# S5 batches of a hybrid decoder step: which engine turns the chunk contributions, and from where

## The chip, the cores and the metric

The kernel runs on one core of a Trainium2 chip. The metric is the device time of one execution, in microseconds (us). All data are fp32; the large products split each operand into a rounded high part and a low rest and take three matmuls per tile.

## The reference

One layer for 1024 prompt tokens and 32 sample tokens: a modulated input goes through `w_in` into five parts; one feeds an RG-LRU, one an S5 state space model, two are gates; then the merge, a norm, a SwiGLU and a norm. The S5 branch, which the change touches, is this (64 groups of 16 channels, 64 complex states each; chunks of the sequence are chained by a scan):

```python
    def body(carry, u_blk):
        hr, hi = carry
        br = jnp.einsum('blgq,gpq->blgp', u_blk, bb_re)
        bi = jnp.einsum('blgq,gpq->blgp', u_blk, bb_im)
        br = br.at[:, 0].add(a_re * hr - a_im * hi)
        bi = bi.at[:, 0].add(a_re * hi + a_im * hr)
        ...
        _, _, xr, xi = lax.associative_scan(_clin_op, (ar, ai, br, bi), axis=1)
        y = jnp.einsum('blgp,gqp->blgq', xr, c_re) - jnp.einsum('blgp,gqp->blgq', xi, c_im)
        return (xr[:, -1], xi[:, -1]), y
```

## The kernel before, in words

**Ticks.** The order of all work is written out by hand. `product` (L346) walks over three column blocks of 352; for each it calls `tick()`, which first runs whatever is due in this tick, then sends 24 matmuls (L342) and hands the PSUM bank to an evacuation. In the stage in question the products are those of `w_in` for the S5 input (evacuated at L456) and for the two gates (evacuated at L861 into one buffer, which a DMA stores).

**The S5 batches.** Eight batches of eight groups run beside these products, on all engines. `S5_PLAN` (L829) lists their steps with the tick in which each is due; batch b begins at tick 3 + 6b, so a new batch starts every six ticks and up to three are under way. Per batch: `s5_const1`, `s5_const2` and `s5_pre1` to `s5_pre4` make the tables and the turned weights (`s5_pre4`: transposes on TensorE L720, copies on ScalarE L722); `s5_turn1` and `s5_turn2` make the table `ee` of a rotation, beginning with ScalarE's L698, and `s5_pe1` (L710, copied at L712) a kernel; `s5_pe2` (L748) makes the chunk contributions, real and imaginary for four pairs of groups, 136 columns each (128 chunks of the prompt, 8 of the samples), in three PSUM banks, which ScalarE copies into `ww` (L751). `s5_rot_in` multiplies them by the rotation's two parts (GpSimd one, VectorE the other), so that a real scan on VectorE (`s5_scan`, L774) can follow; `s5_rot_out` turns the scan's result back in the same way. `s5_states` makes the states, lets ScalarE copy the last of each (`fin`, L793, L794) and stores the others by four DMAs into the operand `xs5` of `s5_pe3` (L811, L812), whose banks `s5_gelu1` and `s5_gelu2` work on.

**Helpers.** All `TENSOR_TENSOR` rows stand at line L117 and all `SCALAR_TENSOR_TENSOR` rows at L126. The split of a weight tile into its two parts is ScalarE's L230 and a GpSimd subtraction (`weights_t<-small_t,weights_t`). In the trace `s_t` and `left_t` are the two memory regions of this stage (`tq`, in which GpSimd's products land, lies in `left_t`; `ww`, `vv`, `ee` in `s_t`), and `ps` is PSUM.

**Banks.** `bank()` hands out the eight PSUM banks in turn. Six ticks take 15: six for products, three each for `s5_pe2` and `s5_pe3`, two for `s5_pre4`, one for `s5_pe1`. The product in the second tick after `s5_pe2`'s tick gets the first bank of `s5_pe2` again.

Of the kernel before, what the change touches and what calls it, by code (L numbers as in the profile page):

```python
# [12 lines left out]
AF = mybir.ActivationFunctionType  # L13
OP = mybir.AluOpType
# [57 lines left out]
def tile_hawk_s5(ctx: ExitStack, tc: tile.TileContext, io):  # L72
    nc = tc.nc
    V, A, P, PE, SP = nc.vector, nc.scalar, nc.gpsimd, nc.tensor, nc.sync
# [50 lines left out]
    def stt(e, out, a, s, b, op0, op1):  # L125
        e.scalar_tensor_tensor(out, a, s, b, op0=op0, op1=op1)  # L126
# [21 lines left out]
    o = 0  # L148
# [15 lines left out]
    fin = cst(2, 32)  # L164
# [263 lines left out]
    s5m = {}  # L428
# [22 lines left out]
    def z_s5_evac(j):  # L451
        def evac(nb, b):
            ze = s5m[f"ze{j % 2}"]
            bias = C["b_in"][:, 16 + j:17 + j]
            n = 44 if nb < 2 else 40
            A.activation(ze[:, :, 8 + 44 * nb:8 + 44 * nb + n].rearrange("p s c -> p c s"),  # L456
                         b[:, :8 * n].rearrange("p (c s) -> p c s", s=8), AF.Identity, bias=bias)
            if nb == 2:
                zs = b[:, 320:352].rearrange("p (q i) -> p i q", i=4)
                A.activation(ze[:, 0:4, 0:8], zs, AF.Identity, bias=bias)  # L460
                A.activation(ze[:, 4:8, 136:144], zs, AF.Identity, bias=bias)
                for s in range(8):
# [274 lines left out]

    groups = ((0, 3), (3, 6), (6, 8))

    def s5_pe2(b):  # L740

        wt, ub, ww = s5m["wt"], s5m["ub"][b % 2], s5m["ww"]
        for n0, n1 in groups:
            wb_ = bank()
            for n in range(n0, n1):
                r, pr = divmod(n, 4)
                for h in range(2):
                    PE.matmul(wb_[64 * h:64 * h + 64, 136 * (n - n0):136 * (n - n0) + 136],  # L748
                              wt[:, 2 * pr + h, 64 * r:64 * r + 64], ub[:, 2 * pr + h, 8:144],
                              start=True, stop=True, skip_group_check=True)  # L750
            A.activation(ww[:, n0:n1], sub(wb_, n1 - n0, 136), AF.Copy)  # L751

    def s5_rot_in(b):

        ww, ws, ee, vv, tq, tv = (s5m[n] for n in ("ww", "ws", "ee", "vv", "tq", "tv"))
        w4 = ww.rearrange("p (r n) c -> p r n c", r=2)
        t = sub(tq, 2, 4, 128)
        for r in (1, 0):
            tt(P, t[:, r], w4[:, r, :, :128], ee[:, 1], OP.mult)
            tt(V, vv[:, r], w4[:, r, :, :128], ee[:, 0], OP.mult)  # L760

    def s5_scan(b):
        ww, ws, vv, tq, tv = (s5m[n] for n in ("ww", "ws", "vv", "tq", "tv"))
        w4 = ww.rearrange("p (r n) c -> p r n c", r=2)
        wf = ww.rearrange("p n c -> p (n c)")
        t = sub(tq, 2, 4, 128)
        A.activation(ws[:, :, 4 * b:4 * b + 4, :], w4[:, :, :, 128:], AF.Copy)
        rr = sub(tv, 4, 128)
        A.activation(rr, over(r8[:, 4 * b:4 * b + 4, None], 4, 128), AF.Copy)
        P.memset(rr[:, :, 0:1], 0.0)  # L770
        tt(V, vv[:, 0], vv[:, 0], t[:, 1], OP.add)
        tt(V, vv[:, 1], vv[:, 1], t[:, 0], OP.subtract)
        for r in range(2):
            V.tensor_tensor_scan(wf[:, 512 * r:512 * r + 512], tv[:, :512],  # L774
                                 vv[:, r].rearrange("p n c -> p (n c)"), 0.0, op0=OP.mult, op1=OP.add)

    def s5_rot_out(b):
        ww, ee, vv, tq, xs5, x0s = (s5m[n] for n in ("ww", "ee", "vv", "tq", "xs5", "x0s"))
        x0s = x0s[b % 2]
        x4 = sub(ww.rearrange("p n c -> p (n c)"), 2, 4, 128)  # L780
        t = sub(tq, 2, 4, 128)
        for r in (1, 0):
            tt(P, t[:, r], x4[:, r], ee[:, 1], OP.mult)
            tt(V, vv[:, r], x4[:, r], ee[:, 0], OP.mult)
        A.activation(xs5[:64, :, 0:8], x0s[:64], AF.Copy)
        A.activation(xs5[64:, :, 0:8], x0s[64:], AF.Copy, scale=-1.0)

    def s5_states(b):
        vv, tq, xs5 = (s5m[n] for n in ("vv", "tq", "xs5"))
        t = sub(tq, 2, 4, 128)  # L790
        tt(V, vv[:, 0], vv[:, 0], t[:, 1], OP.subtract)
        stt(V, vv[:, 1], vv[:, 1], -1.0, t[:, 0], OP.mult, OP.subtract)
        A.activation(fin[:, 0, 4 * b:4 * b + 4], vv[:, 0, :, 127], AF.Copy)  # L793
        A.activation(fin[:, 1, 4 * b:4 * b + 4], vv[:, 1, :, 127], AF.Copy, scale=-1.0)  # L794
        xg = xs5.rearrange("p (n h) c -> p h n c", h=2)
        for r in range(2):
            for h in range(2):
                SP.dma_start(xg[64 * r:64 * r + 64, h, :, 9:136], vv[64 * h:64 * h + 64, r, :, 0:127])

    y_banks = {}  # L800

# [21 lines left out]
    def s5_gelu2(b):  # L823
        gel = s5m["gel"]
        for n0, n1, yv in y_banks.pop(b):
# [3 lines left out]
    S5_PLAN = ((-3, s5_load), (1, s5_const1), (1, s5_pre1), (1, s5_pre2), (2, s5_pre3),  # L829
               (2, s5_load2), (2, s5_const2), (5, s5_turn1), (5, s5_turn2), (5, s5_pe1),  # L830
               (6, s5_k), (6, s5_pre4), (7, s5_pe2), (8, s5_rot_in), (8, s5_toeplitz),
               (9, s5_scan), (10, s5_rot_out), (11, s5_states), (14, s5_pe3), (15, s5_gelu1),
               (16, s5_gelu2))

    def s5_batch(b, first):
# [20 lines left out]
    def merge_evac(d, j, m, st=None):  # L856
        st = s5m["stage"] if st is None else st

        def evac(nb, b):
            s = slice(352 * nb, 352 * nb + 352)  # L860
            A.activation(st[:, s], b[:, :NB], AF.Tanh, bias=bh[:, m - 24:m - 23], scale=0.5)  # L861
            if nb == 2:
                SP.dma_start(d[j], st)
        return evac
# [17 lines left out]
    for k in range(8):  # L882
# [14 lines left out]
        if k in W2_K:  # L897
            i = W2_K.index(k)
# [14 lines left out]
    for j in range(2):  # L913
        e = z_s5_evac(j)
# [48 lines left out]
    def zl_evac(j):  # L963
        def evac(nb, b):
            bias = C["b_in"][:, j:j + 1]
            zs = zl[:, 1027:1083].rearrange("p (s i) -> p s i", i=7)
            n = 352 if nb < 2 else 320
            if nb == 0:
                P.memset(zl[:, 0:3], 0.0)
                P.tensor_copy(zs[:, :, 0:3], C["conv0"][:, j])  # L970
            A.activation(zl[:, 3 + 352 * nb:3 + 352 * nb + n], b[:, :n], AF.Identity, bias=bias)
            if nb == 2:
                ts(V, zs[:, :, 3:7], seqs(b[:, 320:352]), bias, op0=OP.add)
            later(2, lru_conv, j, nb)
            later(3, lru_split, j, nb)
        return evac
# [114 lines left out]
    e = merge_evac(d_tb, 7, 39, zl[:, :T])  # L1091
# [53 lines left out]
    def lru_out_evac(j):  # L1145
        t, m_ = ta_t[j % 2], mo_t[j % 2]

        def evac(nb, b):
            s = slice(352 * nb, 352 * nb + 352)
            stt(V, m_[:, s], t[:, s], 1.0, b[:, :NB], OP.add, OP.mult)  # L1150
            if nb == 2:
                SP.dma_start(d_m[j], m_)
        return evac

    y_load(0)
    for j in range(8):
# [4 lines left out]
        w, e = use_w("lru", j), lru_out_evac(j)  # L1161
# [410 lines left out]
    n1, n2 = plan.emit(1)  # L1572
# [79 lines left out]
    n = len(UNITS)  # L1652
    for u, (j, ss) in enumerate(UNITS):
        bk = {s: {"set": s if len(ss) > 1 else u % 2} for s in ss}
        for v in range(7):
            for s in ss:
# [4 lines left out]
                w, x = parts[7 * u + v], operand(v, s)  # L1661
# [35 lines left out]
    for c, (k0, k1) in enumerate(DOWN[:-1]):  # L1697
        for m in range(8):
# [37 lines left out]
    ws = [next_w("down", (LASTK, m)) for m in range(8)]  # L1736
    for q in ORDQ:
        for m in range(8):
# [3 lines left out]
            b = bank()  # L1742
# [7 lines left out]
    x = M[0]  # L1750
# [150 lines left out]
```

## Time and profile before

| what | value |
|---|---|
| median of 3 runs | 1831.78 us (1830.85 to 1835.74) |
| the profiled execution | 1828.24 us, its span 1826.5 us |
| busy in the span | TensorE 95%, its weight loads 92%, VectorE 64%, ScalarE 39%, GpSimd 56% |
| granted TensorE clock over the span | 0.978 |
| the stage of the S5 batches | about 92 to 376 us of the span |

The shares are averages over stages with different limits. The stage of the S5 batches is a sixth of the span. How its engines wait for one another is read from its own stretch, batch by batch.

### The profile page before, as it was taken

Reading aid. Unit: us, or ns where it says so; the run is one execution under the profiler, and the core shown is the slowest. Engines: PE = TensorE matmul, PEld = TensorE weight load, DVE = VectorE, ACT = ScalarE, POOL = GpSimd, SP = SyncE. Lnnn points to the kernel's source line nnn. Section 1 sums busy time; section 2 is a strip of 40 time slices with the busy share of each in tenths; the row PEclk is TensorE's granted clock in tenths of the full one; section 3 lists DMA queues with packets and bytes.
Section 4 is the critical chain, followed back from the end, with each engine's and each line's share of the span. In section 5 each row is a group of like instructions: output and inputs, shape, how many; then the busy total and the mean of one; then the engine's idle time right before and its main releaser. Section 6 shows DMA issues by size and latency. Waiting matters only on the chain.

```text
span 1826.5 us, 33873 instructions
## 1 busy us (share of the span) xinstructions
PE 1726.6 (95%) x13380; PEld 1687.1 (92%) x13380; DVE 1161.9 (64%) x1946; ACT 719.0 (39%) x1448; POOL 1021.5 (56%) x839
## 2 busy tenths in 40 slices
PE   6999999999878889999999998999999999999996
PEld 5989889999878889999999998999999999999996
DVE  6989999837888853322677577345455545543588
ACT  4433333325555453222345355335433332211244
POOL 3566656435765742255758725567777675222654
PEclk9999999999989999999999999999999999999998
DMA  9335444432111129765344433432233225932212
GB/s 352 102 106 150 155 130 146 142 111 74 61 40 51 49 79 243 233 234 203 114 163 148 135 105 106 139 119 95 95 126 110 95 95 225 368 125 75 82 35 62
DMA packets 118639, 240.93 MB, mean 132 GB/s; under 512 B 23120, under 2 KB 62288, under 8 KB 115408
## 3 DMA queue, kind: packets, MB, share of 16 engines
q1 hardware_dynamic: 118480, 238.76, 39.5%
q8 instruction: 105, 1.72, 0.4%
q14 instruction: 54, 0.44, 0.1%
HBM read 179.59 MB, written 54.97 MB: 128 GB/s over the span
## 4 chain that ended last, share of the span: by engine, by line
PE 64%; DVE 14%; POOL 9%; issue 6%; DMA 3%; ACT 2%; SPq 0%; POOLq 0%; DVEq 0%; ACTq 0%
PE ps L1174 36%; PE ps L342 13%; PE ps L1693 12%; DVE s_t L117 7%; POOL weights_t L117 3%; POOL r_t L117 3%; POOL lru_t L117 2%; DVE left_t L117 1%; DVE s_t L774 1%; DVE rear_t L117 1%; DMA ada_w_t<-in_w_ada_dram 1%; PE ps L401 1%; DVE s_t L126 1%; DMA small_t<-in_w_in_dram 1%; PE ps L748 1%
## 5 line engine op out<-in xcount | busy, mean ns | idle before, releaser
L1174 PE MATMUL ps<-r_t,weights_t 128*128 128x264 f32 x5496 | 683.4, 285 | 10.4 <-POOL weights_t L117 7.9
L1174 PEld LDWEIGHTS ps<-r_t,weights_t 128*128 128x128 f32 x5496 | 672.6, 188 | 16.8 <-POOL weights_t L117 9.9
L117 POOL TENSOR_TENSOR weights_t<-small_t,weights_t 128x512 fp32r<-128x512 f32 (+3 forms) x312 | 395.5, 1283 | 438.1 <-ACT weights_t L230 358.9
L342 PE MATMUL ps<-r_t,weights_t 128*128 128x352 f32 x3384 | 574.1, 330 | 1.5 <-ACT weights_t L230 1.1
L342 PEld LDWEIGHTS ps<-r_t,weights_t 128*128 128x128 f32 x3384 | 556.5, 194 | 11.2 <-issue 7.3
L230 ACT ACTIVATE weights_t<-small_t 128x512 fp32r<-128x512 f32 (+3 forms) x286 | 151.4, 572 | 245.8 <-PE ps L1693 95.3
L126 DVE SCALAR_TENSOR_TENSOR rear_t<-ps,small_t,rear_t 128x264 f32<-128x264 f32 (+1 forms) x192 | 92.5, 482 | 122.8 <-PE ps L1693 95.4
L1693 PE MATMUL ps<-r_t,weights_t 128*128 128x264 f32 x1344 | 166.3, 286 | 4.1 <-ACT weights_t L230 3.3
L1693 PEld LDWEIGHTS ps<-r_t,weights_t 128*128 128x128 f32 x1344 | 165.1, 190 | 5.2 <-ACT weights_t L230 3.5
L117 DVE TENSOR_TENSOR small_t<-ps,small_t 128x264 f32<-128x264 f32 (+1 forms) x228 | 84.8, 379 | 102.4 <-ACT small_t L1618 74.5
L126 DVE SCALAR_TENSOR_TENSOR rear_t<-rear_t,ps 128x264 f32<-128x264 f32 (+1 forms) x74 | 33.2, 457 | 174.1 <-PE ps L1174 95.2
L117 DVE TENSOR_TENSOR s_t<-s_t 128x128 f32<-128x128 f32 (+3 forms) x200 | 134.3, 719 | 11.5 <-ACT s_t L751 5.8
L117 POOL TENSOR_TENSOR r_t<-rear_t,r_t 128x264 fp32r<-128x264 f32 (+2 forms) x77 | 96.9, 1262 | 59.5 <-ACT r_t L1189 22.7
L117 DVE TENSOR_TENSOR rear_t<-rear_t,small_t 128x32 f32<-128x32 f32 (+3 forms) x137 | 97.3, 719 | 41.0 <-POOL weights_t L117 30.9
L117 POOL TENSOR_TENSOR rear_t<-rear_t,small_t 128x264 f32<-128x264 f32 (+1 forms) x108 | 90.9, 863 | 54.6 <-ACT small_t L1237 44.3
L117 POOL TENSOR_TENSOR weights_t<-rear_t,weights_t 128x512 fp32r<-128x512 f32 x57 | 75.2, 1323 | 55.9 <-ACT weights_t L1534 55.9
L126 DVE SCALAR_TENSOR_TENSOR lru_t<-lru_t 128x1056 f32<-128x1056 f32 (+1 forms) x52 | 81.8, 1574 | 29.7 <-ACT lru_t L1012 16.3
L117 POOL TENSOR_TENSOR r_t<-small_t,r_t 128x528 fp32r<-128x528 f32 (+1 forms) x58 | 78.7, 1366 | 35.8 <-ACT r_t L209 25.8
L1693 PE MATMUL ps<-r_t 128*128 128x264 f32 x768 | 96.7, 286 | 0.8 <-POOL r_t L117 0.8
L1693 PEld LDWEIGHTS ps<-r_t 128*128 128x128 f32 x768 | 94.6, 188 | 1.7 <-POOL r_t L117 1.2
L126 DVE SCALAR_TENSOR_TENSOR lru_t<-lru_t,small_t 128x352 f32<-128x352 f32 (+2 forms) x96 | 87.9, 915 | 3.4
L117 POOL TENSOR_TENSOR left_t<-s_t 128x512 f32<-128x512 f32 (+1 forms) x40 | 76.9, 1944 | 5.9 <-DVE s_t L117 3.5
(225 smaller groups left out, 1920.5 us busy)
## 6 DMA issues: line engine op xcount, KB each, us to landing
d_f<-r_t SPq DMA_DIRECT2D x44, 528.0 KB
r_t<-d_f SPq DMA_DIRECT2D x22, 1056.0 KB
small_t<-in_w_up_dram SPq DMA_DIRECT2D x43, 512.0 KB
small_t<-in_w_in_dram SPq DMA_DIRECT2D x40, 512.0 KB
small_t<-in_w_ada_dram SPq DMA_DIRECT2D x32, 512.0 KB
small_t<-in_w_glu_dram SPq DMA_DIRECT2D x32, 512.0 KB
ada_w_t<-in_w_ada_dram SPq DMA_DIRECT2D x16, 512.0 KB
small_t<-in_w_out_dram SPq DMA_DIRECT2D x16, 512.0 KB
```

What stands on the lines that cost most here:

```text
L117: e.tensor_tensor(out, a, b, op=op)
L126: e.scalar_tensor_tensor(out, a, s, b, op0=op0, op1=op1)
L230: A.activation(self.hi[:, s], self.raw[:, s], AF.Copy)
L342: PE.matmul(out[:, :NB], a[:, k, :], x[:, h, nb, k, :], start=bool(first and n == 0 and q == 0), stop=bool(last and n == len(kts) - 1 and ...
L401: PE.matmul(b[32 * j:32 * j + 32, :128], silu_c[:, 2 * i + k, :], w.raw[:, k, 128 * j:128 * j + 128], start=i == k == 0, stop=i == 3 and k ...
L748: PE.matmul(wb_[64 * h:64 * h + 64, 136 * (n - n0):136 * (n - n0) + 136], wt[:, 2 * pr + h, 64 * r:64 * r + 64], ub[:, 2 * pr + h, 8:144], ...
L774: V.tensor_tensor_scan(wf[:, 512 * r:512 * r + 512], tv[:, :512], vv[:, r].rearrange("p n c -> p (n c)"), 0.0, op0=OP.mult, op1=OP.add)
L1174: PE.matmul(out[:, :Q], a[:, k, :], x(h, k), start=bool(first and n == 0 and q == 0), stop=bool(last and n == len(kts) - 1 and q == 2), sk ...
L1693: PE.matmul(b[:, :Q], a[:, n, :], f[:, h, Q * q:Q * q + Q], start=n == i == 0, stop=k == k1 - 1 and i == 2)
```

## The change

Three things in the S5 branch. `s5_pe2` no longer copies its banks to `ww`; ScalarE copies only the eight sample columns of each into `ws` (L756 of the changed kernel), and `s5_rot_in` has VectorE multiply the other 128 columns straight from the banks. So that real and imaginary parts lie as a bank needs them, the banks hold the pairs (real 0 to 2), (imaginary 0 to 2) and (real 3, imaginary 3). `s5_rot_out` puts its two products of GpSimd on VectorE. And the copies of the final states become a step of their own, `s5_fin`, due at tick 12 in place of 11.

```diff
     def s5_pe2(b):
 
-        wt, ub, ww = s5m["wt"], s5m["ub"][b % 2], s5m["ww"]
-        for n0, n1 in groups:
+        wt, ub, ws = s5m["wt"], s5m["ub"][b % 2], s5m["ws"]
+        w_banks[b] = []
+        for i, pairs_ in enumerate((((0, 0), (0, 1), (0, 2)), ((1, 0), (1, 1), (1, 2)), ((0, 3), (1, 3)))):
             wb_ = bank()
-            for n in range(n0, n1):
-                r, pr = divmod(n, 4)
+            for n, (r, pr) in enumerate(pairs_):
                 for h in range(2):
-                    PE.matmul(wb_[64 * h:64 * h + 64, 136 * (n - n0):136 * (n - n0) + 136],
+                    PE.matmul(wb_[64 * h:64 * h + 64, 136 * n:136 * n + 136],
                               wt[:, 2 * pr + h, 64 * r:64 * r + 64], ub[:, 2 * pr + h, 8:144],
                               start=True, stop=True, skip_group_check=True)
-            A.activation(ww[:, n0:n1], sub(wb_, n1 - n0, 136), AF.Copy)
+            x = sub(wb_, len(pairs_), 136)
+            w_banks[b].append(x[:, :, :128])
+            dst = ws[:, i, 4 * b:4 * b + 3, :] if i < 2 else ws[:, :, 4 * b + 3, :]
+            A.activation(dst, x[:, :, 128:], AF.Copy)
 
     def s5_rot_in(b):
...
-        for r in (1, 0):
-            tt(P, t[:, r], w4[:, r, :, :128], ee[:, 1], OP.mult)
-            tt(V, vv[:, r], w4[:, r, :, :128], ee[:, 0], OP.mult)
+        for i, x in enumerate(w_banks.pop(b)):
+            for o, e in ((t, 1), (vv, 0)):
+                if i < 2:
+                    tt(V, o[:, i, :3], x, ee[:, e, :3], OP.mult)
+                else:
+                    tt(V, o[:, :, 3], x, over(ee[:, e, 3, None, :], 2, 128), OP.mult)
 
     def s5_scan(b):
...
-        A.activation(ws[:, :, 4 * b:4 * b + 4, :], w4[:, :, :, 128:], AF.Copy)
...
@@ s5_rot_out
         for r in (1, 0):
-            tt(P, t[:, r], x4[:, r], ee[:, 1], OP.mult)
+            tt(V, t[:, r], x4[:, r], ee[:, 1], OP.mult)
             tt(V, vv[:, r], x4[:, r], ee[:, 0], OP.mult)
...
@@ s5_states
-        A.activation(fin[:, 0, 4 * b:4 * b + 4], vv[:, 0, :, 127], AF.Copy)
-        A.activation(fin[:, 1, 4 * b:4 * b + 4], vv[:, 1, :, 127], AF.Copy, scale=-1.0)
...
+    def s5_fin(b):
+        vv = s5m["vv"]
+        A.activation(fin[:, 0, 4 * b:4 * b + 4], vv[:, 0, :, 127], AF.Copy)
+        A.activation(fin[:, 1, 4 * b:4 * b + 4], vv[:, 1, :, 127], AF.Copy, scale=-1.0)
...
-               (9, s5_scan), (10, s5_rot_out), (11, s5_states), (14, s5_pe3), (15, s5_gelu1),
+               (9, s5_scan), (10, s5_rot_out), (11, s5_states), (12, s5_fin), (14, s5_pe3), (15, s5_gelu1),
```

VectorE's order at the turn in of a batch, as a difference (the last of `s5_const1` above it, the first of `s5_const2` below):

```order
 L117 TENSOR_TENSOR s_t<-left_t,small_t 128x128 x2
 L117 TENSOR_TENSOR s_t<-s_t 128x128
-L117 TENSOR_TENSOR s_t<-s_t 128x512 x2
+L117 TENSOR_TENSOR left_t<-ps,s_t 128x384
+L117 TENSOR_TENSOR s_t<-ps,s_t 128x384
+L117 TENSOR_TENSOR left_t<-ps,s_t 128x384
+L117 TENSOR_TENSOR s_t<-ps,s_t 128x384
+L117 TENSOR_TENSOR left_t<-ps,s_t 128x2x128
+L117 TENSOR_TENSOR s_t<-ps,s_t 128x2x128
 L117 TENSOR_TENSOR left_t<-left_t,s_t 128x1152
```

Six products that read a PSUM bank stand where two that read SBUF stood; at the turn out, likewise, four 512-column products on VectorE stand for two.

GpSimd's order over one batch, from the memset of one scan (L770) to that of the next, before:

```order
L770 MEMSET s_t 128x4
L117 TENSOR_TENSOR weights_t<-small_t,weights_t 128x512 x2
L117 TENSOR_TENSOR left_t<-s_t 128x512 x2
L117 TENSOR_TENSOR weights_t<-small_t,weights_t 128x512 x2
L117 TENSOR_TENSOR s_t<-s_t 128x1024
L117 TENSOR_TENSOR left_t<-s_t 128x1024
L117 TENSOR_TENSOR left_t<-s_t 128x512 x2
L117 TENSOR_TENSOR s_t<-s_t,left_t 128x1024
L770 MEMSET s_t 128x4
```

and in the changed kernel:

```order
L775 MEMSET s_t 128x4
L117 TENSOR_TENSOR weights_t<-small_t,weights_t 128x512 x4
L117 TENSOR_TENSOR s_t<-s_t 128x1024
L117 TENSOR_TENSOR left_t<-s_t 128x1024
L117 TENSOR_TENSOR s_t<-s_t,left_t 128x1024
L775 MEMSET s_t 128x4
```

The four 512-column products of the turns are gone; `s5_pre1`, `s5_pre2` and `s5_pre3` (the three of 1024 columns) now follow one another directly.

ScalarE's order from the evacuation of tick 10 to L722, before:

```order
L861 ACTIVATE left_t<-ps,small_t 128x352
L793 ACTIVATE small_t<-s_t 128x4
L794 ACTIVATE small_t<-s_t 128x4
L698 ACTIVATE s_t<-left_t 128x8x16
L712 ACTIVATE s_t<-ps 128x2x128
L861 ACTIVATE left_t<-ps,small_t 128x352
L722 ACTIVATE s_t<-ps 128x512 x2
```

and in the changed kernel:

```order
L869 ACTIVATE left_t<-ps,small_t 128x352
L698 ACTIVATE s_t<-left_t 128x8x16
L712 ACTIVATE s_t<-ps 128x2x128
L869 ACTIVATE left_t<-ps,small_t 128x352
L805 ACTIVATE small_t<-s_t 128x4
L806 ACTIVATE small_t<-s_t 128x4
L722 ACTIVATE s_t<-ps 128x512 x2
```

The two copies of the final states (L793 and L794 before, L805 and L806 now) moved behind L698, L712 and an evacuation; they still stand ahead of L722.

## Rows read from the trace of the kernel before

**Rows 1.** Chain of waits, 180 to 262 us, its shares by line.

```profile
by line: DVE s_t L117 51.8%; issue 15.6%; DVE left_t L117 14.2%; DVE s_t L774 12.4%; DVE s_t L126 6.6%; ACT s_t L698 0.7%; POOL s_t L770 0.3%; POOLq L117 0.2%; DVEq L117 0.1%; POOLq L770 0.1%; ACT small_t L794 0.1%; ACTq L861 0.0%
```

**Rows 2.** Stretches of a batch: length; busy PE, PEld, DVE, ACT, POOL; PEclk; DMA.

```profile
155.56:187.66 32.10, 30.60 (x234) 29.64 (x233) 31.25 (x42) 10.63 (x29) 21.70 (x11) 1.00 0.52 154
...
257.65:291.90 34.25, 32.27 (x233) 31.14 (x232) 33.19 (x46) 12.32 (x33) 21.57 (x12) 0.95 0.46 145
...
sum 239.37, PE 222.69 PEld 214.63 DVE 226.19 ACT 87.80 POOL 144.38; mean PE 31.81 PEld 30.66 DVE 32.31 ACT 12.54 POOL 20.63
```

**Rows 3.** Waits of TensorE, 92 to 376 us: total, times, longest.

```profile
PE ps L748 <- ACT s_t L722: 14.4, 7, 2.7
...
PE ps L720 <- DVE s_t L126: 1.9, 2, 1.3
PE ps L812 <- DMA s_t<-s_t: 1.5, 2, 1.1
```

**Rows 4.** Waits of VectorE, 92 to 376 us.

```profile
DVE s_t L117 <- ACT s_t L698: 3.3, 7, 0.5
```

**Rows 5.** Timeline of TensorE in two batches: start, length, and idle time before.

```profile
166.45 2.10 PE L748 MATMUL ps<-s_t 128*64 128x136 f32 x32 [1.50 <-ACT s_t L722]
...
262.96 4.08 PE L342 MATMUL ps<-r_t,weights_t 128*128 128x352 f32 x24
269.02 2.67 PE L748 MATMUL ps<-left_t,s_t 128*64 128x136 f32 x32 [1.98 <-ACT s_t L722]
271.62 5.09 PE L342 MATMUL ps<-r_t,weights_t 128*128 128x352 f32 x24
```

**Rows 6.** Timeline, 228 to 256 us: turn out, turn in, `s5_const2`, a product.

```profile
228.43 3.32 DVE L117 TENSOR_TENSOR s_t<-s_t 128x512 f32<-128x512 f32 x2
...
243.91 3.11 DVE L117 TENSOR_TENSOR s_t<-s_t 128x512 f32<-128x512 f32 x2
244.07 2.40 POOL L117 TENSOR_TENSOR left_t<-s_t 128x1024 f32<-128x1024 f32 x1 [0.23 <-DVE s_t L117]
...
246.02 11.70 PE L342 MATMUL ps<-r_t,weights_t 128*128 128x352 f32 x72
...
246.94 2.44 DVE L117 TENSOR_TENSOR left_t<-left_t,s_t 128x1152 f32<-128x1152 f32 x1
...
250.50 3.50 POOL L117 TENSOR_TENSOR s_t<-s_t,left_t 128x1024 f32<-128x1024 f32 x1
251.78 3.43 DVE L117 TENSOR_TENSOR left_t<-left_t,s_t 128x1152 f32<-128x1152 f32 x1
...
255.14 1.40 DVE L126 SCALAR_TENSOR_TENSOR s_t<-s_t,ps 128x408 f32<-128x408 f32 x3
```

**Rows 7.** Timeline: VectorE alone, and reading PSUM beside GpSimd's split.

```profile
84.14 1.35 DVE L117 TENSOR_TENSOR s_t<-left_t,s_t 128x1152 f32<-128x1152 f32 x1
...
222.31 1.28 DVE L117 TENSOR_TENSOR s_t<-s_t,left_t 128x512 f32<-128x512 f32 x2
...
226.08 2.19 POOL L117 TENSOR_TENSOR weights_t<-small_t,weights_t 128x512 fp32r<-128x512 f32 x1
227.12 1.39 DVE L126 SCALAR_TENSOR_TENSOR s_t<-s_t,ps 128x408 f32<-128x408 f32 x3
```

**Rows 8.** Line L117, 765 to 1550 us: ns at least, median and most.

```profile
L117 DVE TENSOR_TENSOR small_t<-ps,small_t x191: 176/433/437, 1026.8 to 1549.2; 128x264 f32<-128x264 f32 x180, 128x32 f32<-128x32 f32 x11
...
L117 DVE TENSOR_TENSOR small_t<-small_t,rear_t x28: 434/436/1498, 884.7 to 1068.8; 128x264 f32<-128x264 f32 x28
```

**Rows 9.** Timeline of ScalarE, 230 to 237 us.

```profile
232.58 0.21 ACT L793 ACTIVATE small_t<-s_t 128x4 f32<-128x4 f32 x1 [4.64 <-DVE s_t L117]
...
233.30 0.29 ACT L698 ACTIVATE s_t<-left_t 128x128 f32<-128x128 f32 x1
...
234.20 1.08 ACT L722 ACTIVATE s_t<-ps 128x512 f32<-128x512 f32 x2
```

**Rows 10.** Busy time just behind the stage.

```profile
375.00:408.00 33.00, 33.00 (x226) 32.58 (x224) 16.50 (x31) 10.12 (x23) 9.16 (x11) 1.00 0.30 107
```

More of the change, by code (lines that the diff above doesn't have):

```diff
@@ L738, in tile_hawk_s5 @@
     groups = ((0, 3), (3, 6), (6, 8))
+    w_banks = {}
     def s5_pe2(b):
-        wt, ub, ww = s5m["wt"], s5m["ub"][b % 2], s5m["ww"]
-        for n0, n1 in groups:
+        wt, ub, ws = s5m["wt"], s5m["ub"][b % 2], s5m["ws"]
+        w_banks[b] = []
+        for i, pairs_ in enumerate((((0, 0), (0, 1), (0, 2)), ((1, 0), (1, 1), (1, 2)), ((0, 3), (1, 3)))):
             wb_ = bank()
-            for n in range(n0, n1):
-                r, pr = divmod(n, 4)
+            for n, (r, pr) in enumerate(pairs_):
                 for h in range(2):
-                    PE.matmul(wb_[64 * h:64 * h + 64, 136 * (n - n0):136 * (n - n0) + 136],
+                    PE.matmul(wb_[64 * h:64 * h + 64, 136 * n:136 * n + 136],
                               wt[:, 2 * pr + h, 64 * r:64 * r + 64], ub[:, 2 * pr + h, 8:144],
                               start=True, stop=True, skip_group_check=True)
-            A.activation(ww[:, n0:n1], sub(wb_, n1 - n0, 136), AF.Copy)
+            x = sub(wb_, len(pairs_), 136)
+            w_banks[b].append(x[:, :, :128])
+            dst = ws[:, i, 4 * b:4 * b + 3, :] if i < 2 else ws[:, :, 4 * b + 3, :]
+            A.activation(dst, x[:, :, 128:], AF.Copy)
     def s5_rot_in(b):
-        ww, ws, ee, vv, tq, tv = (s5m[n] for n in ("ww", "ws", "ee", "vv", "tq", "tv"))
-        w4 = ww.rearrange("p (r n) c -> p r n c", r=2)
+        ee, vv, tq = (s5m[n] for n in ("ee", "vv", "tq"))
         t = sub(tq, 2, 4, 128)
-        for r in (1, 0):
-            tt(P, t[:, r], w4[:, r, :, :128], ee[:, 1], OP.mult)
-            tt(V, vv[:, r], w4[:, r, :, :128], ee[:, 0], OP.mult)
+        for i, x in enumerate(w_banks.pop(b)):
[4 more added lines that the diff above has]
+                    tt(V, o[:, :, 3], x, over(ee[:, e, 3, None, :], 2, 128), OP.mult)
     def s5_scan(b):
-        ww, ws, vv, tq, tv = (s5m[n] for n in ("ww", "ws", "vv", "tq", "tv"))
-        w4 = ww.rearrange("p (r n) c -> p r n c", r=2)
+        ww, vv, tq, tv = (s5m[n] for n in ("ww", "vv", "tq", "tv"))
         wf = ww.rearrange("p n c -> p (n c)")
         t = sub(tq, 2, 4, 128)
-        A.activation(ws[:, :, 4 * b:4 * b + 4, :], w4[:, :, :, 128:], AF.Copy)
         rr = sub(tv, 4, 128)
```

## The prediction

> **What bounds the kernel now.** The page's shares (TensorE 95%, VectorE 64%) say little here, since the change lies in one stage only: the 61 ticks in which TensorE works off products of `w_in` while the eight batches of the S5 branch run beside them, from about 92 to 376 us. So I read that stage, in four steps.
>
> First the chain of waits inside it. From 180 to 262 us it hardly touches TensorE: nearly nine tenths are VectorE's lines, and most of the rest is "issue" [rows 1]. So in this stage VectorE sets the pace, not TensorE.
>
> Then the period of one batch (six ticks), taken from one `s5_pe1` on TensorE to the next. It is 34.25 us at 257.65, of which VectorE is busy for 33.19, and the seven periods in a row sum to 239.37 [rows 2]. The cheapest one, at 155.56, is 32.10 us at a granted clock of 1.00, with one wait of 1.50 in it [rows 2, 5]. Without that wait TensorE needs **30.6 us** per batch: that is its floor.
>
> Third, where TensorE loses the difference. It waits in front of `s5_pe2` (L748) for ScalarE's copy of the turned weights (L722): 14.4 us in seven waits, beside 1.9 us at L720 and 1.5 us at L812 [rows 3]. A second loss follows the wait in five of the seven periods: after 1.98 us of idling the 32 matmuls of L748 take 2.67 instead of 2.10 and the next product 5.09 instead of 4.08 [rows 5], with a mean granted clock of 0.95 in that period against 1.00 [rows 2]. [...] That is 1.6 us each time. Seven floors are 7 x 30.6 = 214.2, so the seven periods hold 239.37 - 214.2 = 25.2 us that VectorE causes; with the 1.1 us or so at the last `s5_pe3` (of the 1.5 at L812) some **26.3 us** are to be had. No more: then TensorE is at its own work.
>
> Fourth, why ScalarE is late and why VectorE is slow. ScalarE stands for 4.64 us at L793, the copy of the final states, until VectorE has made them; L698, L712 and L722 queue behind it, so L722 starts at 234.20 [rows 9]. VectorE is slow because GpSimd holds it up: while GpSimd's 1024-column product runs from 244.07 for 2.40, two 512-column products on VectorE take 3.11 from 243.91 [rows 6]; two of that size with no GpSimd work beside them take 1.28 [rows 7]. But a VectorE instruction that reads one operand from PSUM isn't held: three of them go through in 1.39 from 227.12 while GpSimd's from 226.08 lasts until 228.27 [rows 7], and over 191 PSUM products in the later stages the longest is 437 ns, where the same shape from SBUF has a median of 436 and a longest of 1498 [rows 8].
>
> **The change part by part**, per batch, in VectorE's time.
>
> Turn in (`s5_rot_in`). Before: from 243.91 to 246.94, 3.0 us, for two products, GpSimd doing two others [rows 6]. After: six products from PSUM, 2 x (384 + 384 + 256) columns. The trio of 408, 408 and 272 columns takes 1.39 [rows 7], so 1024 of 1088 columns make 1.31, twice 2.6 us. Gain 0.4. That they aren't held is the step I rest on; if they were, one hold by a 1024-column GpSimd product, 3.11 - 1.28 = 1.8, comes back. Ends: gain 0.4, loss 1.4; I take the gain, by rows 7 and 8.
>
> `s5_const2` behind it. Before: three 1152-column products take from 246.94 to 255.14, 8.2 us, each with a hold: two by GpSimd's turn-in products, one by `s5_pre3` (250.50, 3.50) [rows 6]. Alone, one takes 1.35 at 84.14 [rows 7], three about 3.9. After, GpSimd's queue has nothing between `s5_pre2` and `s5_pre3`, so the latter, 3.50 - 1.28 = 2.2 of own work (from 250.50 it waits until VectorE is through with its second, at 251.78), can hold one of them at most: 3.9 + 2.2 = 6.1. Gain 2.1; ends 0 (all held as now) and 4.3 (`s5_pre3` done in time).
>
> Turn out (`s5_rot_out`). Before: 3.32 us from 228.43, for two products and two holds [rows 6]. After: four at 1.28 per two [rows 7], 2.5. Gain 0.8. If the weight split's two GpSimd products now fall beside them, about 1.1 each is lost.
>
> Final states a tick later. `s5_turn1` no longer waits for L698 behind L793: 3.3 us in seven waits [rows 4], 0.5 per batch. L805 and L806 now stand just ahead of L722, so L722 still waits for the states, but L698, L712 and one evacuation are out of its way: from 233.30 to 234.20, 0.9 us [rows 9].
>
> ScalarE's three copies of `ww` (some 1.3 us) and L767 become three copies of a few columns. ScalarE isn't the bound: nothing in the sum. GpSimd loses four products: nothing either, but for the holds above.
>
> Sum: 0.4 + 2.1 + 0.8 + 0.5 = 3.8 us, so VectorE's period falls from 34.2 to **30.4**, just under TensorE's 30.6. TensorE then sets the pace. One link keeps VectorE from drawing far ahead: `s5_const2` writes the buffer `vx` that `s5_pe3` of the same tick still reads. It costs nothing while TensorE is the bound.
>
> The banks of `s5_pe2` are held longer: VectorE frees them, not ScalarE. TensorE takes the first of them again for the product two ticks on. VectorE began its turn in at about 243.91, and that product starts about 249.8 (a third of the 72 matmuls that take 11.70 from 246.02) [rows 6]: room for 2.6 us of work.
>
> Of the 26.3 us I give back one wait of the present mean size, 14.4 / 7 = 2.1 us, for the first batches, where VectorE starts late, as an estimate: 24.2. The profiled execution took 1828.24, so 1804.0; the median of the runs stands 3.5 above it: 1831.78 - 24.2 = **1807.6 us**.
>
> [...] For 264 columns the rows show no surcharge: median 433 ns from PSUM, 436 from SBUF [rows 8]. [...]
>
> **The rivals.**
> *VectorE stays the bound.* If one hold stays (a PSUM product held after all, or both split products beside the turn out), VectorE's period is 30.4 + 2.0 = 32.4. Saved: 7 x 1.8 + 1 = 14 us, 1818. With both it is 34.4 and nothing is saved. For it: the two engines' periods differ by 0.2 only. Against: rows 8.
> *Given back.* The stage ends earlier, and something that doesn't move takes it all. From 375 to 408 TensorE is busy for 33.00 of 33.00 us [rows 10] with loads well ahead, so I see no such thing; 1831.
> *Slower.* The holds don't go with GpSimd's products: VectorE finds the remaining ones (`s5_pre1` to `s5_pre3`, four of the split) in its way as long as now, while it has 2.6 us more of its own work: two more products of 0.64 and 2.6 - 1.3 for the turn in. With 0.5 for L698 off, its period is 34.2 + 2.1 = 36.3, and seven of them make 15 us: 1847. It decides where the holds that vanish are worth under 2.1 us per batch; by the terms above they are 8.2 - 6.1 = 2.1 in `s5_const2`, 3.32 - 1.28 = 2.0 in the turn out and 1.8 in the turn in, 5.9 in all.
>
> **How the numbers follow.** TensorE at its floor, 1802 to 1812: 0.72. VectorE still the bound, 1812 to 1824: 0.17. Given back: 0.06. Slower: 0.05. Under 0.3%, 5.5 us, a measurement of this kernel can't be told from no change: faster 0.89, same 0.06, slower 0.05. The range from 1801 to 1820 takes in the first case and two thirds of the second.
>
> **What would show it.** Right: periods of 30.6 to 31 us between `s5_pe1` groups, L748's wait gone, granted clock 1.00, six PSUM products at 0.4 to 0.56 us each, one hold among the three 1152-column products. Wrong: PSUM products of 2 us and more, the split beside the turn out, periods over 32, or a new TensorE wait for VectorE at the product two ticks after `s5_pe2`.

## The result, and the profile after

The changed kernel takes **1803.93 us** (median, 1802.32 to 1806.26) against 1831.32 for the kernel before on the same chip: a ratio of 0.9849 (95% interval 0.9826 to 0.9872), 1.5% faster. The forecast was 1807.6 in a range of 1801 to 1820. The execution that was profiled took 1803.03 us, its span 1801.3, against 1828.24 and 1826.5 before.

Stretches of a batch in the changed kernel, from one `s5_pe1` to the next (columns as in [rows 2]); the seventh holds the end of the batches:

```profile
121.08:151.56 30.48, 30.48 (x234) 29.64 (x233) 29.69 (x50) 13.54 (x34) 13.77 (x9) 1.00 0.56 142
151.56:182.04 30.48, 30.48 (x233) 29.64 (x232) 29.02 (x51) 11.36 (x30) 13.39 (x10) 1.00 0.57 162
...
243.01:273.50 30.49, 30.49 (x233) 29.65 (x232) 28.97 (x52) 11.16 (x30) 12.62 (x9) 1.00 0.55 159
...
sum 213.15, PE 213.15 PEld 207.48 DVE 194.70 ACT 80.82 POOL 84.87; mean PE 30.45 PEld 29.64 DVE 27.81 ACT 11.55 POOL 12.12
```

TensorE is busy in every one of the 213.15 us; the seven periods of [rows 2] took 239.37 and held 222.69 us of its work, in five of them at a mean granted clock of 0.95. Now the granted clock is 1.00 in all seven. So 26.2 us are gone between the two `s5_pe1` that bound the sums. In the first six periods VectorE was busy for 33.2 us each before, and is for 29.2 now. Before, these six sum to:

```profile
sum 205.41, PE 190.68 PEld 183.55 DVE 199.21 ACT 74.25 POOL 129.48; mean PE 31.78 PEld 30.59 DVE 33.20 ACT 12.38 POOL 21.58
```

The chain of waits, 180 to 262 us, of which VectorE's lines were 85% [rows 1], is now:

```profile
by line: PE ps L342 74.1%; PE ps L750 7.3%; PE ps L819 6.8%; PE ps L820 6.6%; PE ps L720 3.2%; PE ps L710 2.1%
```

All of it is TensorE's own work. Of TensorE's waits from 92 to 376 us one is left, at the start of the stage, where the kernel before has one of 4.4:

```profile
PE ps L710 <- DVE s_t L117: 4.5, 1, 4.5
```

None of the three groups of waits that cost the kernel before its time [rows 3] has a row any more. VectorE waits instead; its waits from 155 to 300 us:

```profile
DVE s_t L117 <- ACT s_t L698: 2.9, 3, 1.5
DVE left_t L117 <- PE ps L820: 2.0, 3, 0.9
DVE s_t L117 <- PE ps L820: 0.3, 1, 0.3
```

The second and third are the link through `vx` that the forecast named: `s5_const2` writes what `s5_pe3` (L819, L820 now) still reads. The place that decides, the turn in and `s5_const2` behind it, with GpSimd's work beside them, against [rows 6]; and further up in the same batch what became of the holds at the weight split (rows of VectorE and GpSimd alone; a hold is an instruction of VectorE that is drawn out by GpSimd's work beside it):

```profile
223.15 3.00 POOL L117 TENSOR_TENSOR weights_t<-small_t,weights_t 128x512 fp32r<-128x512 f32 x2 [8.74 <-ACT weights_t L230]
...
223.76 1.25 DVE L117 TENSOR_TENSOR s_t<-s_t 128x128 f32<-128x128 f32 x1
...
228.38 0.29 DVE L117 TENSOR_TENSOR s_t<-s_t 128x128 f32<-128x128 f32 x1
228.59 0.55 DVE L117 TENSOR_TENSOR left_t<-ps,s_t 128x384 f32<-128x384 f32 x1
228.75 2.03 POOL L117 TENSOR_TENSOR left_t<-s_t 128x1024 f32<-128x1024 f32 x1 [0.55 <-DVE s_t L117]
229.06 0.55 DVE L117 TENSOR_TENSOR s_t<-ps,s_t 128x384 f32<-128x384 f32 x1
...
230.45 0.41 DVE L117 TENSOR_TENSOR left_t<-ps,s_t 128x256 f32<-128x256 f32 x1
230.78 0.41 DVE L117 TENSOR_TENSOR s_t<-ps,s_t 128x256 f32<-128x256 f32 x1
230.86 2.39 POOL L117 TENSOR_TENSOR s_t<-s_t,left_t 128x1024 f32<-128x1024 f32 x1
231.67 2.80 DVE L117 TENSOR_TENSOR left_t<-left_t,s_t 128x1152 f32<-128x1152 f32 x1 [0.47 <-PE ps L820]
234.39 1.35 DVE L117 TENSOR_TENSOR s_t<-left_t,s_t 128x1152 f32<-128x1152 f32 x1
235.77 1.36 DVE L117 TENSOR_TENSOR left_t<-left_t,s_t 128x1152 f32<-128x1152 f32 x1
237.05 1.41 DVE L126 SCALAR_TENSOR_TENSOR s_t<-s_t,ps 128x408 f32<-128x408 f32 x3
```

The six PSUM products run from 228.59 to about 231.2, 2.6 us, while GpSimd's 1024-column product (`s5_pre2`, 228.75) runs beside them from end to end: none is held. Of the three 1152-column products one is held, by `s5_pre3` (230.86); from the first to the next instruction is 5.4 us, 8.2 before; 0.47 us of waiting for `s5_pe3` stand ahead of it. The weight split (223.15) now stands beside the small products of `s5_const1`: one of 128 columns takes 1.25 us there, where another of the same size takes 0.29 at 228.38. That hold has moved, not gone: before, it lay at `s5_turn1` and `s5_turn2`, which took 6.8 us up to `s5_const1` and take 4.7 in this batch.

### The profile page after: what moved, and what is told of

The parts are those of the page before. It is cut to its first block, busy times and chain, and to the rows that moved or that the text cites. A ratio compares the mean times of both kernels' runs of the same rounds, so it can differ in the third digit from the quotient of the medians.

```text
span 1801.3 us, 33909 instructions
## 1 busy us (share of the span) xinstructions
PE 1718.6 (95%) x13380; PEld 1681.3 (93%) x13380; DVE 1131.2 (63%) x1994; ACT 711.6 (40%) x1440; POOL 954.9 (53%) x807
## 4 chain that ended last, share of the span: by engine, by line
PE 73%; POOL 9%; DVE 7%; issue 5%; DMA 2%; ACT 2%; SPq 0%; POOLq 0%; DVEq 0%; ACTq 0%
PE ps L1182 36%; PE ps L342 20%; PE ps L1701 12%; POOL weights_t L117 3%; POOL r_t L117 3%; POOL lru_t L117 2%; DVE rear_t L117 2%; DVE s_t L117 1%; PE ps L750 1%; PE ps L820 1%; PE ps L819 1%; PE ps L401 1%; DVE small_r_t L486 1%; DMA small_t<-in_w_down_dram 1%; DVE small_t L117 1%
## 5 line engine op out<-in xcount | busy, mean ns | idle before, releaser
L1182 PE MATMUL ps<-r_t,weights_t 128*128 128x264 f32 x5496 | 683.8, 285 | 10.2 <-POOL weights_t L117 6.7
L117 POOL TENSOR_TENSOR weights_t<-small_t,weights_t 128x512 fp32r<-128x512 f32 (+3 forms) x312 | 395.0, 1281 | 472.4 <-ACT weights_t L230 387.3
L342 PE MATMUL ps<-r_t,weights_t 128*128 128x352 f32 x3384 | 569.5, 328 | 1.9 <-ACT weights_t L230 1.1
L342 PEld LDWEIGHTS ps<-r_t,weights_t 128*128 128x128 f32 x3384 | 551.6, 192 | 10.8 <-issue 7.1
L117 DVE TENSOR_TENSOR small_t<-ps,small_t 128x264 f32<-128x264 f32 (+1 forms) x228 | 84.7, 378 | 102.3 <-ACT small_t L1626 74.5
L126 DVE SCALAR_TENSOR_TENSOR rear_t<-rear_t,ps 128x264 f32<-128x264 f32 (+1 forms) x74 | 33.3, 457 | 173.5 <-PE ps L1182 96.7
L117 POOL TENSOR_TENSOR r_t<-rear_t,r_t 128x264 fp32r<-128x264 f32 (+2 forms) x77 | 96.7, 1260 | 59.4 <-ACT r_t L1197 22.7
L117 DVE TENSOR_TENSOR rear_t<-rear_t,small_t 128x32 f32<-128x32 f32 (+3 forms) x137 | 97.3, 719 | 41.1 <-POOL weights_t L117 31.0
L117 POOL TENSOR_TENSOR rear_t<-rear_t,small_t 128x264 f32<-128x264 f32 (+1 forms) x108 | 90.7, 862 | 54.6 <-ACT small_t L1245 44.3
L117 POOL TENSOR_TENSOR weights_t<-rear_t,weights_t 128x512 fp32r<-128x512 f32 x57 | 75.3, 1326 | 56.2 <-ACT weights_t L1542 49.0
L117 POOL TENSOR_TENSOR r_t<-small_t,r_t 128x528 fp32r<-128x528 f32 (+1 forms) x58 | 78.7, 1367 | 35.9 <-ACT r_t L209 26.0
L1701 PE MATMUL ps<-r_t 128*128 128x264 f32 x768 | 96.7, 286 | 0.8 <-POOL r_t L117 0.8
L117 DVE TENSOR_TENSOR s_t<-s_t 128x128 f32<-128x128 f32 (+4 forms) x184 | 73.9, 445 | 5.2 <-ACT s_t L698 2.9
L1182 PE MATMUL ps<-r_t 128*128 128x264 f32 x600 | 76.7, 283 | 0.0
```

Source lines behind the costliest of these rows:

```text
L342: PE.matmul(out[:, :NB], a[:, k, :], x[:, h, nb, k, :], start=bool(first and n == 0 and q == 0), stop=bool(last and n == len(kts) - 1 and ...
L1182: PE.matmul(out[:, :Q], a[:, k, :], x(h, k), start=bool(first and n == 0 and q == 0), stop=bool(last and n == len(kts) - 1 and q == 2), sk ...
L1701: PE.matmul(b[:, :Q], a[:, n, :], f[:, h, Q * q:Q * q + Q], start=n == i == 0, stop=k == k1 - 1 and i == 2)
```

## The experiments

**One part at a time.** The change has three parts: A, the turn in straight from PSUM; B, the turn out on VectorE alone; C, the final states copied a tick later. Each was run without the other two. A alone is the changed kernel with these lines back:

```diff
-            tt(V, t[:, r], x4[:, r], ee[:, 1], OP.mult)
+            tt(P, t[:, r], x4[:, r], ee[:, 1], OP.mult)
...
-  (11, s5_states), (12, s5_fin),
+  (11, s5_states), (11, s5_fin),
```

B alone is the kernel before with the first line of these as in the changed kernel (and `s5_fin` as a step of its own, still at tick 11), C alone with the second.

> Only the turn in from PSUM on VectorE; GpSimd keeps its turn-out products, the final states are copied at tick 11. Holds theory: of 3.8 us per batch this part carries 2.5 (turn in 0.4, s5_const2 2.1), so VectorE stays the bound at a period of about 31.7 us, and the kernel takes about 1813 us. Rival (ScalarE's queue: what matters is L722 behind the final states): this part gives only the 1.3 us of copies on ScalarE, period over 33, about 1826 us.

> Only the turn out on VectorE alone. Holds theory: 0.8 us per batch, period 33.4, about 1826 us. Rival (VectorE's own work counts, not the holds): two more 512-column products cost 1.3 us per batch, period 35.5, about 1840 us.

> Only the copies of the final states a tick later. Holds theory: VectorE remains the bound and gets back its 0.5 us wait for L698, period 33.7, about 1828 us. Rival (ScalarE's queue): the 14.4 us of TensorE's waits for L722 and the time at the lower clock behind them go with it, period about 31.5, about 1812 us.

Measured: A alone 1808.87 us (ratio 0.9881, 0.9865 to 0.9898), B alone 1821.42 (0.9944, 0.9929 to 0.9959), C alone 1825.53 (0.9969, 0.9957 to 0.9981). Their mean periods over the same six batches are 30.99, 33.08 and 33.38 us; the kernel before has 34.24. The waits in front of `s5_pe2` stay with B and C alone (10.2 and 9.8 us in seven, from 14.4); with A alone 1.8 in three are left. So A is the part that carries the result, as the forecast's sum has it (2.5 of its 3.8 us), and every part gives something by itself, each more than its term: 3.25, 1.16 and 0.86 us of period against 2.5, 0.8 and 0.5. All three came out faster than expected, by 2.5 to 4.6 us. A part of the excess lies in the earliest of the six periods. From the start of one batch's turn out on VectorE to that of the next, from 185 us on, are 34.2 us in the kernel before and 31.3, 33.3 and 33.5 with A, B and C alone: 2.9, 0.9 and 0.7 us are gained.

**Two parts at a time.** The three pairs:

> Turn in and turn out as changed, the final states copied at tick 11 as before. Holds theory: VectorE at 34.2 - 0.4 - 2.1 - 0.8 = 30.9, within 0.5 us of TensorE's floor, so nearly the whole gain: 1804 to 1808 us. Rival (ScalarE's queue): L722 still stands behind the final states with all its waits, so TensorE still waits some 2 us per batch: 1820 us or more.

> The changed kernel with the turn out on VectorE and GpSimd again (turn in from PSUM and final states at tick 12 as changed). By the prediction's steps: with the turn in alone VectorE's period was 31.0 us; taking L698 and the final states off it is worth some 0.5, so the period comes to 30.5 and the time to 1803 to 1806: then either of the two other parts, added to the turn in, is enough. Rival (the later final states are worth something only while VectorE has more than TensorE's work per batch in other places too): the period stays at 30.9 to 31.0 and the time at 1807 to 1810.

> The turn out on VectorE alone and the final states at tick 12, the turn in as before the change (ScalarE copies the banks, GpSimd makes one of the products). Alone these two parts gave periods of 33.1 and 33.4 us against 34.2. If what they save adds up, the period is 34.2 - 1.2 - 0.9 = 32.2 to 32.4 and the time 1814 to 1818: the turn in from PSUM is then the one part without which TensorE's own pace isn't reached. Rival (any two parts are enough, as with the turn in and either of the others): periods of 30.5 to 31 and 1802 to 1808.

| parts | time, us | ratio (95%) | mean period, us |
|---|---|---|---|
| A + B | 1802.32 | 0.9841 (0.9827 to 0.9856) | 30.49 |
| A + C | 1804.79 | 0.9853 (0.9836 to 0.9869) | 30.69 |
| B + C | 1816.07 | 0.9911 (0.9895 to 0.9928) | 32.45 |
| A + B + C (the change) | 1803.93 | 0.9849 (0.9826 to 0.9872) | 30.48 |

B and C add up (1.16 + 0.86 = 2.0; together 34.24 - 32.45 = 1.8) and don't reach TensorE's pace. A with either of the two does, within 0.2 us of period. Whether C is worth anything with A and B there was asked once more, the two kernels side by side:

> Turn in from PSUM and turn out on VectorE, final states at tick 11 as before the change. Beside the changed kernel on the same chip: if the later final states are worth nothing once the other two parts are there, the two times lie within 1.5 us of each other. Rival: the later final states are worth 2 us or more and the earlier pair of runs, taken apart, hid it.

> The changed kernel itself beside the two others: 1802 to 1806, periods of 30.5 us.

A + B took 1803.10 us (1800.44 to 1803.35), all three parts 1803.83 (1801.19 to 1805.57); both have TensorE's 4.6 us at L710 as their only wait in the stage. **The later copy of the final states is worth nothing in the changed kernel that four runs of each can show**, though alone it gave 0.3%.

**Is it PSUM, or that VectorE does all of it?** Here ScalarE copies the banks to `ww` as before, and VectorE makes all four products of the turn in from there; the rest is as changed:

```diff
         for r in (1, 0):
-            tt(P, t[:, r], w4[:, r, :, :128], ee[:, 1], OP.mult)
+            tt(V, t[:, r], w4[:, r, :, :128], ee[:, 1], OP.mult)
             tt(V, vv[:, r], w4[:, r, :, :128], ee[:, 0], OP.mult)
```

> As the changed kernel, but ScalarE copies the banks to ww as before and VectorE's turn in reads ww: four 512-column products from SBUF in place of six from PSUM, nothing for GpSimd. Holds theory: the products themselves cost the same 2.5 us, but one of them is now held by GpSimd's 1024-column product for 1.8 to 2.0 us, so VectorE's period rises from about 29.3 of work to about 31.2, over TensorE's 30.5: 0.7 us in each of seven periods, 1806 to 1811 us, with one of the four products at over 2 us. Rival (it is the engine that counts, not where the operand lies): no held product, 1804 us.

It took 1812.07 us (0.989, 0.9875 to 0.9905), a little over the range expected, with a period of 31.62. Its turn in on the timeline, and its waits of TensorE:

```profile
266.12 0.68 DVE L117 TENSOR_TENSOR left_t<-s_t 128x512 f32<-128x512 f32 x1
...
266.27 2.40 POOL L117 TENSOR_TENSOR left_t<-s_t 128x1024 f32<-128x1024 f32 x1 [0.23 <-DVE s_t L117]
266.72 2.51 DVE L117 TENSOR_TENSOR s_t<-s_t 128x512 f32<-128x512 f32 x1
...
268.75 2.73 POOL L117 TENSOR_TENSOR s_t<-s_t,left_t 128x1024 f32<-128x1024 f32 x1
...
269.15 2.88 DVE L117 TENSOR_TENSOR left_t<-s_t 128x512 f32<-128x512 f32 x1
271.96 0.68 DVE L117 TENSOR_TENSOR s_t<-s_t 128x512 f32<-128x512 f32 x1
...
272.56 2.62 DVE L117 TENSOR_TENSOR s_t<-left_t,s_t 128x1152 f32<-128x1152 f32 x2
```

```profile
PE ps L815 <- DMA s_t<-s_t: 5.3, 5, 1.4
...
PE ps L748 <- ACT s_t L722: 1.2, 2, 0.9
```

Same GpSimd work beside it, same arithmetic, but from SBUF: two of the four products are held and the turn in takes 6.4 us instead of 2.6. One hold was expected; there are two, since the first makes the turn in long enough to meet `s5_pre3` as well. In return `s5_const2` meets none (1.3 us each). This prices the operand's place by itself: reading PSUM directly is worth about 1.1 us of period and 7 to 8 us of time here, because GpSimd's work doesn't draw those products out: in the batch shown of the changed kernel the six take 0.41 to 0.55 us each, while two of these four take 2.51 and 2.88 and the other two 0.68. ScalarE's copies are back too, but from 150 to 300 us VectorE has no row of waiting for them. In VectorE's own time the price is about 2 us per batch (turn in and `s5_const2` together 10.4 us, against 2.5 + 5.9 where VectorE doesn't wait); TensorE's floor hides the rest. This kernel differs from B + C by GpSimd's products of the turn in alone: taking those off GpSimd brought the period from 32.45 to 31.62, and the operand in PSUM from there to 30.48.

**How much spare does VectorE have?** The turn out's first product is done over, once (two more instructions per batch) and twice (four more):

```diff
             tt(V, t[:, r], x4[:, r], ee[:, 1], OP.mult)
+            tt(V, t[:, r], x4[:, r], ee[:, 1], OP.mult)
             tt(V, vv[:, r], x4[:, r], ee[:, 0], OP.mult)
```

> As the changed kernel, with two of the turn-out products done twice: 1.2 us more on VectorE per batch, same results. By the prediction's sum (VectorE 30.4 against TensorE 30.5) the period becomes 31.6 and the time about 1812 us. By the trace of the changed kernel (VectorE busy 29.0 to 29.7 in each period of 30.48) it just fits: 1804 to 1807 us.

> As the changed kernel, with the turn-out products done four times in excess: 2.4 us more on VectorE per batch. By the prediction's sum the period becomes 32.8, about 1820 us. By the trace of the changed kernel 29.3 + 2.4 = 31.7, 1.2 us over TensorE's in seven periods: about 1812 us. If VectorE no longer mattered at all: 1804 us.

They took 1808.32 us (0.9869, 0.9855 to 0.9884) and 1820.08 (0.9935, 0.9919 to 0.9952), with mean periods of 30.87 and 32.34. The first lies between its two forecasts (1812, and 1804 to 1807). The second hits 1820, the figure by the prediction's sum, but by two errors that cancel: both expectations priced an added product at 0.6 us, and on the timeline it is 0.73, while the sum has VectorE's own work too high. In the second kernel the turn out reads:

```profile
220.47 2.13 DVE L117 TENSOR_TENSOR left_t<-s_t 128x512 f32<-128x512 f32 x3
222.52 0.69 DVE L117 TENSOR_TENSOR s_t<-s_t 128x512 f32<-128x512 f32 x1
223.12 2.14 DVE L117 TENSOR_TENSOR left_t<-s_t 128x512 f32<-128x512 f32 x3
225.18 0.69 DVE L117 TENSOR_TENSOR s_t<-s_t 128x512 f32<-128x512 f32 x1
...
225.90 0.69 DVE L117 TENSOR_TENSOR s_t<-s_t,left_t 128x512 f32<-128x512 f32 x1
```

From 220.47 to 225.90 is 5.43 us; the four products of the changed kernel take 2.52, so 2.9 us were added, and 1.45 with half as many. VectorE's own period is read between its own marks, the starts of two turns out in a row. In the kernel with four more the next one starts at 253.03; of the other kernel two are shown:

```profile
253.03 2.13 DVE L117 TENSOR_TENSOR left_t<-s_t 128x512 f32<-128x512 f32 x3
```

```profile
217.42 1.41 DVE L117 TENSOR_TENSOR left_t<-s_t 128x512 f32<-128x512 f32 x2
...
248.52 1.41 DVE L117 TENSOR_TENSOR left_t<-s_t 128x512 f32<-128x512 f32 x2
```

That is 32.56 and 31.10 us. Without the added work VectorE needs 32.56 - 2.91 = 29.65 and 31.10 - 1.45 = 29.65 us per batch: the two agree. (The mean periods of TensorE give 29.4, but they hold early batches in which VectorE isn't behind yet, and three of the six with two more are TensorE's own 30.5.) **VectorE has 0.8 us of spare under TensorE's 30.5**, four times the 0.2 that was forecast; with more on it the old wait is back:

```profile
PE ps L750 <- ACT s_t L722: 7.8, 7, 1.7
...
PE ps L822 <- DMA s_t<-s_t: 4.4, 5, 1.8
```

**A try at going further.** With the S5 stage at TensorE's pace, the largest waits left stand in the RG-LRU stage, 380 to 760 us. Here the low part of the third column block is made by VectorE, ahead of the scan, instead of GpSimd:

```diff
-            later(3, lru_split, j, nb)
+            if nb < 2:
+                later(3, lru_split, j, nb)
+            else:
+                todo[now[0] + 3].insert(0, (lru_split, (j, nb, V)))
```

> As the changed kernel, and in the RG-LRU stage behind it the low part of the last column block (lru_split of block 2) is made by VectorE ahead of the scan, in place of GpSimd behind the scan and behind two copies of the scan's last columns. Holds theory carried over: TensorE waits 5 to 6 us for this subtraction at the gates (L1019, 20.7 us for GpSimd in seven waits and more for ScalarE); VectorE can have it ready some 3 us earlier, so 15 to 22 us less: 1782 to 1789 us. Rival (VectorE's scan comes later by the subtraction and its wait for ScalarE, and the stage's VectorE chain takes it all back): 1804 us or more.

It took 1805.19 us (0.9851, 0.9836 to 0.9866): nothing gained. TensorE's waits from 380 to 760 us in the changed kernel, and then in this one:

```profile
PE ps L1019 <- POOL r_t L117: 20.7, 7, 3.4
PE ps L1019 <- ACT r_t L1003: 9.7, 6, 1.6
```

```profile
PE ps L342 <- ACT lru_t L979: 20.8, 6, 3.9
PE ps L1022 <- ACT r_t L1006: 3.5, 6, 1.6
...
PE ps L342 <- ACT lru_t L869: 3.3, 1, 3.3
```

The wait at the gates did go, from 30.4 us to 3.5. But TensorE now waits at L342 instead, for ScalarE's evacuation L979: 20.8 us, and 3.3 for L869. L979 comes no sooner: at its wait it stands behind ScalarE's L1059, which waits up to 0.8 us for VectorE behind the moved product, and from one such evacuation to the next are 34.1 us, 33.9 in the changed kernel. So the wait has moved and the pace of the stage hasn't changed, as the rival expected. What is left would be 30.4 - 27.6 = 2.8 us, of which the time shows none. What sets that pace was not followed up.

## Why the prediction was right

The likeliest case came true, in the way that was described: VectorE falls below TensorE's pace, the wait at `s5_pe2` (14.4 us in seven) and the lower clock behind it (0.95 in five periods of seven, 1.00 in all now) go together, and TensorE sets the time of the stage. By its steps:

**The floor and what was to be had.** Right, to 1.0 us. 30.6 per batch was read off one period by taking its one wait off; measured it is 30.48 (213.15 in seven, 214.2 forecast). The last `s5_pe3` lost its wait about as forecast (1.1): from its first matmul's start to its last's 5.0 us before, 4.0 now.

**The turn in.** 2.6 us forecast, 2.6 measured, and the step that it rested on, that PSUM products aren't held, holds in all eight batches: the 48 products take 0.40 to 0.56 us each, whichever of them GpSimd runs beside. The copy to SBUF first is what the experiment from `ww` does, and that kernel is 7 to 8 us slower than the change. No surcharge for the PSUM read shows: from one product's start to the next's are 0.47 us for 384 columns, 0.60 for 512 from SBUF, about the same per column (1.22 and 1.17 ns), and at one size [rows 8] has no difference (medians of 433 and 436 ns).

**`s5_const2`.** 6.1 us forecast, 5.9 measured where VectorE comes to it without a wait, as in the batch before the one shown above:

```profile
201.34 4.61 DVE L117 TENSOR_TENSOR s_t<-left_t,s_t 128x1152 f32<-128x1152 f32 x2
205.98 1.36 DVE L117 TENSOR_TENSOR s_t<-s_t 128x1152 f32<-128x1152 f32 x1
207.26 1.41 DVE L126 SCALAR_TENSOR_TENSOR s_t<-s_t,ps 128x408 f32<-128x408 f32 x3
```

One hold, by `s5_pre3`, as said, at 2.0 us instead of 2.2. In the batch above it is 5.4, since 0.47 us of `s5_pre3` pass while VectorE waits for `s5_pe3`; wait and step together are 5.85. Where the sum was silent is the first batch: there all three products are held, 9.2 us (108.33 to 117.50), and TensorE has no wait from it.

**The turn out.** 2.5 us forecast; 2.5 measured in four of the eight batches (the four products from 214.56 to 217.08, say). In the other four the weight split falls beside them and they take 3.5 to 4.5 us, which the forecast had named with about 1.1 per hold and left out of the sum. In the four good batches this pair of split products stands beside the scan just ahead; the second pair of each batch stands at `s5_const1` or just ahead of it, as above, a place for which the sum had no line; it costs there what it cost at `s5_turn1` and `s5_turn2` before. Where TensorE sets the pace, VectorE's spare covers both.

**Final states a tick later.** This step failed as a term of the sum. 0.5 us per batch was about right where VectorE is the bound: with C alone the wait at L698 is gone (0 from 155 to 300 us, 1.9 in four before), and VectorE's own period is 0.7 shorter. In the changed kernel it is back, up to 1.5 us long and 2.9 in three, and harmless: VectorE arrives early and waits for a ScalarE that itself waits for TensorE:

```profile
248.25 0.56 ACT L869 ACTIVATE left_t<-ps,small_t 128x352 f32<-128x352 f32 x1 [6.80 <-PE ps L720]
248.70 0.30 ACT L698 ACTIVATE s_t<-left_t 128x128 f32<-128x128 f32 x1
```

**VectorE's period.** 30.4 forecast, 29.65 measured by the two kernels with added work. This is the term that was mis-sized, by about 0.75 us, and not in one step: set against the kernel before, step by step, `s5_const2` gave 2.3 us (2.1 forecast), the turn in 0.5 (0.4), the turn out 0.9 (0.8), the way from the turn out to `s5_const1`, with the wait for L698 in it, 0.7 (0.5), and the two additions ahead of the scan 0.1, which the sum doesn't have. The forecast left 0.2 us between the two engines, and so a chance of 0.17 for VectorE as the bound; the margin is 0.8.

**What is given back.** This term was wrong in its place and about right in its size. 2.1 us were taken off for the first batches; there nothing was lost. Set matmul by matmul against the kernel before, the changed execution is 0.4 us behind when the stage begins and still at 125 us; at the end of the stage it is 26.9 us ahead (forecast: 26.3). Then it loses 0.6 at 692 us of the kernel before, 0.2 at 806, and 0.9 from 1540 to 1571. What took these 1.7 us was not followed up. The two profiled executions end 25.2 us apart (24.2 forecast).

**The distance of the median.** Of the 3.7 us between 1807.6 and 1803.93, 1.0 is the saving; the other 2.6 is no step of the kernel: the median before stood 3.5 us above the profiled execution, and that distance was carried over; after the change it is 0.9.

The rivals fell by the experiments: "slower" needed the holds to stay, and the holds of the turn in went with A; "given back" needed something downstream that takes it all, and 1.7 us were taken.

## What to carry to other kernels

When an engine is slowed by another one beside it, look in the trace for instructions of the slowed engine that are not slowed in the same place, and ask what differs: here it was one operand in PSUM (0.41 to 0.55 us beside GpSimd's product, against 2.51 and 2.88 from SBUF), and moving the operand was worth more than sharing the work (a period of 30.48 us, against 32.45 with B and C, where GpSimd makes its half of the turn in). Price a change of several parts against the point where the next engine becomes the bound: one part brought the period within 0.5 us of TensorE's floor, either of the other two closed most of the rest, and the third one then bought nothing, though it measures well alone. And read the margin of an engine between its own marks, while it is the slower one: periods taken on the other engine mix in stretches in which that one set the pace.

## What the runs showed of the hardware

One hold led to the next: from `ww` the first held product pushed the turn in into the following GpSimd product, which held a second one (2.51 and 2.88 us instead of 0.68). In two rows the held product ends a little less than its own length after GpSimd's: in that kernel at 269.23, 0.56 us after GpSimd's end at 268.67; in the changed one the held 1152-column product at 234.47, 1.22 us after 233.25 (0.68 and 1.35 are their lengths alone). So in these rows a hold costs about what is left of GpSimd's instruction. And the lower clock came with the waits: before, four of the first six periods have a mean granted clock of 0.95, and the wait in front of `s5_pe2` is 2.1 us on average [rows 2, 3]. With B or C alone that wait is 1.4 to 1.5 us on average, and all six periods of each have 1.00:

```profile
sum 198.45, PE 184.93 PEld 177.68 DVE 192.66 ACT 71.97 POOL 111.06; mean PE 30.82 PEld 29.61 DVE 32.11 ACT 12.00 POOL 18.51
```

```profile
sum 200.27, PE 186.01 PEld 178.18 DVE 196.91 ACT 72.09 POOL 129.43; mean PE 31.00 PEld 29.70 DVE 32.82 ACT 12.02 POOL 21.57
```

(the six periods of B alone, then of C alone). TensorE's busy time per period falls from 31.8 us to 30.8 and 31.0, without any change to TensorE's work. The length of this one wait doesn't decide it alone: single waits of 2.15 us before, 2.18 with B and 2.12 with C stand in periods at 1.00, waits of 1.95 and 1.98 before in periods at 0.95. What else decides is open. How much of the gain of B and C in TensorE's periods comes back through this was not separated: VectorE's busy time fell too, from 33.2 to 32.1 and 32.8.
